# Two-layer hybrid decoder: gating products on another engine, two recurrence heads at priority, weight sums one set at a time

## The chip, the cores and the metric

The kernel runs on one core of a Trainium2 chip. The metric is the time of one execution on the device in microseconds (us). A core has a matrix engine (TensorE, PE), a vector engine (VectorE, DVE), a scalar engine (ScalarE, ACT), a general engine (GpSimd, POOL) and a queue engine that starts transfers (SyncE, SP). Each takes its instructions in the order of the program and waits on semaphores for the others.

## The reference

Two layers on 1024 rows of width 1024. Layer 0 is windowed attention; layer 1 is a gated linear recurrence (HGRN2) with eight heads of 128. The change lies in layer 1:

```python
h = rmsnorm(x, pre_norm_w[layer])
proj = h @ w_in                                   # 1024 x 4096
q, f, i, z = jnp.split(proj, ...)                 # 1024 columns each
q = silu(q)
log_f = logaddexp(log(lb), log1p(-lb) + log_sigmoid(f)); k = -expm1(log_f)
o = chunked_gated_recurrence(q, k, i, log_f)      # per head: state S, 128 x 128
o = o * rsqrt(mean(o * o, -1) + eps) * gnorm_w
o = o * silu(z)                                   # the gate
x = x + rmsnorm(o @ w_out, post_norm_w[layer])
```

## The kernel before

Every fp32 product is three products of split operands (high x high, low x high, high x low), all by `product` (L246). Weights come from DRAM through `fetch` (L162, on SP, four staging tiles `wraw`); `advance` splits each as soon as one of ten slots is free: the high part `whi` on ACT (L203), the low part `wlo` on DVE (L204).

Layer 1 has two parts. `mixer1` projects the values `i` (`i_unit`, halves 0 and 1), and `q` and `f` head by head (`qf_unit`; L946 multiplies `q` by its sigmoid and so empties a PSUM bank), and works the heads off in `rec(h)`: two scans on DVE, scaled copies (L1032, L1035, L1036), scores on PE (`psd`, `pss`, `psq`), transposes that ACT takes from PSUM as `yn` (L1088), products with them (`psk`, L1093), the chain of states `S` on DVE (L1099), the output (`pso`) and its norm.

`final1` computes z and the output projection, each as seven block products (`z1`, `z7`, `z6`, `z4`, `z5`, `z3`, `z2`, and the same for `o`). Four of the seven use sums and differences of weight quarters. These are made in `weight_sums` during `mixer1`, 128 rows at a time: load four quarters `bq`, four operations on DVE, store four results in DRAM (`tz` for z, `td` for the output); there are four sets of each. From there they are fetched like weights. The first z block (`first_part`, into the tiles `p1z`) runs within `mixer1`, ahead of head 7. `gate` multiplies one 128x512 block of the recurrence's output by silu(z): the silu on ACT (L1236), the product on POOL (L1237), 16 times. `turned` transposes the gated blocks on PE (L1208), `split` makes high and low parts for the output projection (ACT L1200, DVE L1201).

The order on each engine is set when the program is built, by a scheduler with a simulated time line, from the order in which `plan` calls the units and from priorities. Instructions of different units are interleaved by it.

Of the kernel before, what the change touches and what calls it, by code (L numbers as in the profile page):

```python
# [12 lines left out]
F32 = mybir.dt.float32  # L13
# [5 lines left out]
ALU = mybir.AluOpType  # L19
# [4 lines left out]
P = 128  # L24
# [66 lines left out]
def emit(tc, I, out):  # L91
    nc = tc.nc
    v = InOrder(tc, nc.vector)
# [7 lines left out]
    with top:  # L101
# [11 lines left out]
        tz, td, sd = [[dp.tile([4 * P, 512], F32, name=f"{n}{i}") for i in range(4)] for n in ("tz", "td", "sd")]  # L113
# [24 lines left out]
        QZ, QO = (100, 108, 104, 112), (120, 128, 116, 124)  # L138
# [15 lines left out]
        W = {"phase": 0, "pos": 0, "bank": 0, "plan": [], "split": 0, "fetch": 0, "left": {}, "place": {}, "dmas": {}, "split_ins": {}, "free": list(zip(whi, wlo))}  # L154
# [767 lines left out]
        def mixer1(fast, vo, rp, p1z):  # L922
            def i_unit(c, t):
                ps = proj_nat(52 if c == 0 else 76, t)
                nc.scalar.activation(vo[c][:, t, :], ps, AF.Copy)
# [8 lines left out]
            def qf_unit(h, isf, half):  # L934
                ps = proj_feat(60 + 4 * h + 2 * isf + 8 * (h // 4), half)
                cs = slice(half * 512, (half + 1) * 512)
                if (h, isf) not in qfk:
                    if isf and fast:
                        qfk[h, 1] = Fs[h % 2]
                    else:  # L940
                        qfk[h, isf] = rp.tile([P, T], F32, tag="qf"[isf], bufs=2 if isf else nb3, name="qf")
                dst = qfk[h, isf][:, cs]
                if not isf:
                    sg = rp.tile([P, 512], F32, tag="sg", bufs=2, name="sg")
                    nc.scalar.activation(sg, ps, AF.Sigmoid)
                    v.tensor_tensor(dst, ps, sg, op=ALU.mult)  # L946
                else:
                    if (h, 2) not in qfk:
                        qfk[h, 2] = rp.tile([P, T], F32, tag="k", bufs=nb3, name="kk")
                    kk = qfk[h, 2][:, cs]  # L950
                    lb, ol = lbt[:, 1, h:h + 1], lbt[:, 0, h:h + 1]
                    nc.scalar.activation(dst, ps, AF.Sigmoid)  # L952
                    nc.scalar.activation(kk, ps, AF.Sigmoid, scale=-1.0)
                    nc.gpsimd.tensor_scalar(dst, dst, ol, lb, op0=ALU.mult, op1=ALU.add)  # L954
                    nc.gpsimd.tensor_scalar(kk, kk, ol, 1.0, op0=ALU.mult, op1=ALU.mult)
# [161 lines left out]
            qf = lambda h: [lambda u=u: qf_unit(h, *u) for u in QF]  # L1117
            iu = lambda c: [lambda t=t: i_unit(c, t) for t in range(8)]

            def weight_sums(k, quarters, dst, neg):  # L1120

                b = [rp.tile([P, 2, 512], F32, tag=t, name="bq") for t in ("yn", "S")]
                b11, b21, b12, b22 = (x[:, i, :] for x in b for i in range(2))
                for q, x in zip(quarters, (b11, b12, b21, b22)):
                    nc.sync.dma_start(x, I["w"][q + k])
                if neg:
                    v.tensor_tensor(b22, b12, b22, op=ALU.subtract)
                else:
                    v.tensor_tensor(b22, b22, b12, op=ALU.subtract)
                v.tensor_tensor(b12, b12, b11, op=ALU.subtract)  # L1130
                v.tensor_tensor(b11, b11, b22, op=ALU.subtract if neg else ALU.add)
                v.tensor_tensor(b21, b21, b11, op=ALU.subtract)
                for d, x in zip(dst, (b22, b11, b21, b12)):
                    nc.sync.dma_start(d[k * P:(k + 1) * P, :], x)

            rc = lambda h: [lambda: rec(h)]

            def with_sums(units, *a):
                ws = [lambda k=k: weight_sums(k, *a) for k in range(4)]
                return units[:1] + ws[:1] + units[1:3] + ws[1:2] + units[3:5] + ws[2:3] + units[5:7] + ws[3:] + units[7:]  # L1140

            def first_parts():
                next_phase()
                for t in range(3):
                    first_part(t, p1z[t])

            plan = iu(0)
            wo = [lambda k=k: weight_sums(k, QO, td, False) for k in range(4)]
            plan = plan[:1] + wo[:1] + plan[1:3] + wo[1:2] + plan[3:5] + wo[2:3] + plan[5:7] + wo[3:] + plan[7:] + qf(0) + ([zeros] if fast else []) + qf(1) + rc(0) + qf(2) + rc(1) + qf(3) + rc(2) + with_sums(iu(1), QZ, tz, True) + rc(3)
            plan += qf(4) + qf(5) + rc(4) + qf(6) + rc(5) + qf(7) + rc(6) + [first_parts] + rc(7)  # L1150
            for u in plan:
                u()
            if fast:
# [23 lines left out]
        def final1(vo, fp, p1z, spare):  # L1177
# [56 lines left out]

            def gate(c, t, z):
                nc.scalar.activation(z, z, AF.Silu)  # L1236
                nc.gpsimd.tensor_tensor(vo[c][:, t, :], vo[c][:, t, :], z, op=ALU.mult)  # L1237

            banks = ["mm", "mm", "s", "s"]

# [13 lines left out]
            for t in range(4):  # L1254
                ps = mm(tag="to"[t % 2])
                part(ps, quad(4, 1), "z4", t, False)

                sg = sgs[t % 2]
                v.tensor_tensor(sg, ps, u3[t], op=ALU.add)
                gate(0, 4 + t, sg)  # L1260
            p53 = []
            for t in range(4):
                p53.append(mm(tag=banks[t]))
                part(p53[t], quad(0, 1), "z5", t, False)

                v.tensor_tensor(u3[t], p53[t], u3[t], op=ALU.add)
                gate(1, 4 + t, u3[t])
                if t > 1:
                    turned(1, (2 * t - 4, 2 * t - 3))
            for t in range(4):  # L1270
                part(p53[t], quad(0, 0), "z3", t, True)

                v.tensor_tensor(p1[t], p53[t], p1[t], op=ALU.add)
                gate(1, t, p1[t])
                if t > 1:
                    turned(1, (2 * t, 2 * t + 1))
# [75 lines left out]
        def network(fast):  # L1352
            keep, oc = layer0()
            with pool("vo", "left") as vp:
                vo = [o0.rearrange("p a (b c) -> p (a b) c", b=2), vp.tile([P, 8, 512], F32, name="vo1")]
                with pool("fin0", "right") as fp:
                    output0(oc, fp, vo[1])
                keep.close()
                with pool("p1z", "right") as zp:
                    p1z = [zp.tile([P, 512], F32, name=f"p1z{t}") for t in range(3)]  # L1360
                    with pool("rec", "left") as rp:
                        final1(vo, rp, p1z, mixer1(fast, vo, rp, p1z))
# [109 lines left out]
```

## Time and profile before

| | us |
|---|---|
| median of three runs | 899.87 (897.39 to 900.57) |
| profiled execution | 900.18 |
| its span (first to last instruction) | 898.4 |
| PE busy | 863.6 (96%) |
| DVE busy | 642.4 (72%) |
| ACT busy | 453.6 (50%) |
| POOL busy | 343.8 (38%) |

Busy times are of the whole span; PE's are pipelined instructions whose ends are modelled. The mean granted clock of PE is 0.986 of full speed. The value projection of layer 1 begins near 400 us, the heads go on to about 755, the z blocks run from about 700 to 800, and the output projection ends the kernel.

### The profile page before, as it was taken

What the parts mean: (1) busy time and instruction counts of PE and PEld (TensorE: products, weight loads), DVE (VectorE), ACT (ScalarE), POOL (GpSimd) and SP (SyncE); (2) the same over time, 40 slices, a digit from 0 to 9 for tenths busy, and PEclk for the clock granted to TensorE, in tenths of its full rate; (3) what the DMA queues carried; (4) which work ended last, traced back from release to release, by engine and by line L of the source; (5) the groups of instructions that cost most, each with busy time, mean ns of one, the idle gap of its engine ahead of it and who ended that gap; (6) DMA issues with size and microseconds to landing.
All of it is one profiled execution on the core that took longest, in us unless ns stands there. A gap on an engine that the chain in (4) does not pass through costs nothing.

```text
span 898.4 us, 14633 instructions
## 1 busy us (share of the span) xinstructions
PE 863.6 (96%) x5166; PEld 716.6 (80%) x5166; DVE 642.4 (72%) x1043; ACT 453.6 (50%) x1143; POOL 343.8 (38%) x491
## 2 busy tenths in 40 slices
PE   6999999999999999999899999999999899996996
PEld 5888888888878788788788888878887688885885
DVE  7998887777898346865488774466767867567885
ACT  5635777767788233843222331343334454574532
POOL 4543545655676203300344422115424421535032
PEclk9999999999999999999999999999999989997999
DMA  9766454322132135447741010670103245312345
GB/s 336 280 197 180 139 167 139 92 80 73 48 98 75 47 95 187 157 163 258 258 147 40 25 49 24 216 253 29 43 25 94 88 149 188 95 59 83 92 124 187
DMA packets 72923, 114.11 MB, mean 127 GB/s; under 512 B 7048, under 2 KB 27144, under 8 KB 72840
## 3 DMA queue, kind: packets, MB, share of 16 engines
q1 hardware_dynamic: 72560, 113.01, 39.2%
q8 instruction: 43, 0.70, 0.3%
q14 instruction: 40, 0.33, 0.1%
q10 hardware_dynamic: 280, 0.07, 0.0%
HBM read 81.76 MB, written 29.46 MB: 124 GB/s over the span
## 4 chain that ended last, share of the span: by engine, by line
PE 74%; DVE 9%; DMA 5%; ACT 4%; POOL 4%; issue 4%; SPq 0%; DVEq 0%; POOLq 0%; ACTq 0%
PE psmm L246 43%; PE psmm L88 17%; PE pss L88 3%; PE pso L88 2%; PE pso L1106 2%; POOL o L1237 2%; DMA bq<-in_w 1%; PE psk L1093 1%; PE pst L88 1%; PE pso L1108 1%; POOL rstd L285 1%; DVE wlo L204 1%; DMA wraw<-tz 1%; ACT whi L203 1%; DMA tz<-bq 1%
## 5 line engine op out<-in xcount | busy, mean ns | idle before, releaser
L246 PE MATMUL psmm<-whi,acth 128*128 128x512 f32 x448 | 177.9, 399 | 1.3 <-DVE y L851 1.3
L246 PE MATMUL psmm<-wlo,acth 128*128 128x512 f32 x448 | 176.1, 393 | 0.0
L246 PE MATMUL psmm<-whi,actl 128*128 128x512 f32 x448 | 174.8, 394 | 0.0
L204 DVE TENSOR_TENSOR wlo<-wraw,whi 128x512 fp32r<-128x512 f32 x144 | 102.2, 724 | 51.8 <-ACT whi L203 46.9
L203 ACT ACTIVATE whi<-wraw 128x512 fp32r<-128x512 f32 x136 | 84.3, 628 | 90.5 <-PE psmm L246 57.9
L88 PE MATMUL psmm<-acth,whi 128*128 128x512 f32 x272 | 110.7, 407 | 1.7 <-ACT whi L88 1.7
L88 PE MATMUL psmm<-acth,wlo 128*128 128x512 f32 x272 | 107.7, 396 | 0.0
L88 PE MATMUL psmm<-actl,whi 128*128 128x512 f32 x272 | 107.3, 395 | 0.2 <-DVE actl L88 0.2
L246 PE MATMUL psmm<-acth,whi 128*128 128x512 f32 x256 | 102.0, 398 | 2.6 <-DVE qf L946 2.6
L246 PE MATMUL psmm<-actl,whi 128*128 128x512 f32 x256 | 101.1, 395 | 0.0
L246 PE MATMUL psmm<-acth,wlo 128*128 128x512 f32 x256 | 100.7, 393 | 0.0
L246 PEld LDWEIGHTS psmm<-whi,acth 128*128 128x128 f32 x448 | 85.0, 190 | 19.4 <-DVE y L851 1.9
L246 PEld LDWEIGHTS psmm<-whi,actl 128*128 128x128 f32 x448 | 84.7, 189 | 17.7
L246 PEld LDWEIGHTS psmm<-wlo,acth 128*128 128x128 f32 x448 | 84.9, 190 | 16.8
L736 ACT ACTIVATE sm<-sm,st 128x129 f32<-128x129 f32 x128 | 49.9, 392 | 26.1 <-DVE st L734 26.0
L88 PEld LDWEIGHTS psmm<-acth,wlo 128*128 128x128 f32 x272 | 51.5, 190 | 11.7 <-DVE wlo L88 0.2
L88 PEld LDWEIGHTS psmm<-acth,whi 128*128 128x128 f32 x272 | 52.0, 191 | 10.3 <-ACT whi L88 2.0
L246 PEld LDWEIGHTS psmm<-acth,whi 128*128 128x128 f32 x256 | 48.4, 189 | 14.1 <-DVE qf L946 4.0
L88 PEld LDWEIGHTS psmm<-actl,whi 128*128 128x128 f32 x272 | 51.9, 191 | 8.7 <-DVE actl L88 0.7
L246 PEld LDWEIGHTS psmm<-acth,wlo 128*128 128x128 f32 x256 | 48.5, 190 | 10.2
L246 PEld LDWEIGHTS psmm<-actl,whi 128*128 128x128 f32 x256 | 48.5, 189 | 9.6
L954 POOL TENSOR_SCALAR gate<-gate,lbt 128x512 f32<-128x512 f32 x16 | 18.5, 1153 | 95.2 <-ACT gate L952 84.6
(334 smaller groups left out, 1773.6 us busy)
## 6 DMA issues: line engine op xcount, KB each, us to landing
wraw<-in_w SPq DMA_DIRECT2D x124, 256.0 KB
QS<-qd SPq DMA_DIRECT2D x16, 512.0 KB
bq<-in_w SPq DMA_DIRECT2D x32, 256.0 KB
xr<-in_x SPq DMA_DIRECT2D x8, 512.0 KB
x1d<-xn SPq DMA_DIRECT2D x8, 512.0 KB
td<-bq SPq DMA_DIRECT2D x16, 256.0 KB
tz<-bq SPq DMA_DIRECT2D x16, 256.0 KB
wraw<-sd SPq DMA_DIRECT2D x16, 256.0 KB
```

Of the source, the lines that this page charges most:

```text
L88: return (lambda *a, **k: self.tc.keep_in_program_order(f(*a, **k))) if self.on else f
L203: nc.scalar.activation(hi, raw, AF.Copy)
L204: W["split_ins"][i] = v.tensor_tensor(lo, raw, hi.bitcast(F32), op=ALU.subtract)
L246: W["mm"] = pe.matmul(ps, a, b, start=(k == first and i == 0), stop=(k == last and i == 2), skip_group_check=first is None)
L285: W["rstd"] = keep(g.tensor_tensor(r, m, nhalf[:, :width], op=ALU.pow))
L736: W["exp"] = nc.scalar.activation(sm[:, h, :], sm[:, h, :], AF.Exp, bias=nm[:, h:h + 1], scale=-1.0, accum_out=dn[:, h:h + 1])
L954: nc.gpsimd.tensor_scalar(dst, dst, ol, lb, op0=ALU.mult, op1=ALU.add)
L1093: nc.tensor.matmul(pk[:, i, :], yn[:, c, :], vt[:, c, hc], start=True, stop=True)
L1106: nc.tensor.matmul(po[:, i, :], sc[:, c, :], vt[:, c, hc], start=True, stop=(c == 0))
L1108: nc.tensor.matmul(po[:, i, :], X[:, c * P:(c + 1) * P], S[:, c, :], start=False, stop=True)
L1237: nc.gpsimd.tensor_tensor(vo[c][:, t, :], vo[c][:, t, :], z, op=ALU.mult)
```

## The change

There are three parts. In `gate` the product goes to DVE. The heads 6 and 7 are built under `tc.high_priority(offset=1200)`, with `first_parts` between them as before. `weight_sums` works on the three tiles `p1z` instead of the tiles of `yn` and `S`, so only three quarters are loaded at first; the fourth goes into the tile of b12 after that has been stored. Each of the eight sets is issued behind the last weight fetch known when it is built (`behind`), and the sets stand elsewhere in the plan: those of z one after each of the projections of heads 1 to 3 and one within the second half of the values, those of the output after that half and after the projections of heads 4 to 6.

```diff
             def weight_sums(k, quarters, dst, neg):
 
-                b = [rp.tile([P, 2, 512], F32, tag=t, name="bq") for t in ("yn", "S")]
-                b11, b21, b12, b22 = (x[:, i, :] for x in b for i in range(2))
-                for q, x in zip(quarters, (b11, b12, b21, b22)):
-                    nc.sync.dma_start(x, I["w"][q + k])
+                b11, b12, b22 = p1z
+                for q, x in zip(quarters, (b11, b12, None, b22)):
+                    if x is not None:
+                        nc.sync.dma_start(x, I["w"][q + k])
...
                 v.tensor_tensor(b12, b12, b11, op=ALU.subtract)
                 v.tensor_tensor(b11, b11, b22, op=ALU.subtract if neg else ALU.add)
+                r = slice(k * P, (k + 1) * P)
+                for d, x in ((3, b12), (0, b22), (1, b11)):
+                    nc.sync.dma_start(dst[d][r], x)
+                b21 = b12
+                nc.sync.dma_start(b21, I["w"][quarters[2] + k])
                 v.tensor_tensor(b21, b21, b11, op=ALU.subtract)
-                for d, x in zip(dst, (b22, b11, b21, b12)):
-                    nc.sync.dma_start(d[k * P:(k + 1) * P, :], x)
+                nc.sync.dma_start(dst[2][r], b21)
...
+            def behind(f, *a):
+
+                with tc.issue_after(W["dmas"][W["fetch"] - 1].ins):
+                    f(*a)
+
+            def ahead(h):
+                with tc.high_priority(offset=1200):
+                    rec(h)
...
+            i1 = iu(1)
+            plan = iu(0) + qf(0) + ([zeros] if fast else []) + qf(1) + wz[:1] + rc(0) + qf(2) + wz[1:2] + rc(1) + qf(3) + wz[2:3]
+            plan += rc(2) + i1[:4] + wz[3:] + i1[4:] + wo[:1] + rc(3) + qf(4) + wo[1:2] + qf(5) + wo[2:3] + rc(4) + qf(6)
+            plan += wo[3:] + rc(5) + qf(7) + [lambda: ahead(6), first_parts, lambda: ahead(7)]
...
             def gate(c, t, z):
                 nc.scalar.activation(z, z, AF.Silu)
-                nc.gpsimd.tensor_tensor(vo[c][:, t, :], vo[c][:, t, :], z, op=ALU.mult)
+                v.tensor_tensor(vo[c][:, t, :], vo[c][:, t, :], z, op=ALU.mult)
```

Below `weight_sums` the lines of the kernel after stand 11 higher.

On ACT, at head 6 of the recurrence, before the change: `yn_6972` is the first eviction of head 6, `whi4` and `whi5` are splits of z weights that come from `tz` (an underscore and a number mark the copy of a tile).

```order
L203 ACTIVATE acth3_0_128<-wraw3_115 128x512
L1175 ACTIVATE pair_7288<-psmm_7301 128x512
L203 ACTIVATE whi4_96<-wraw0_112 128x512
L203 ACTIVATE whi5_97<-wraw1_113 128x512
L1246 ACTIVATE pair_7288<-psmm_7345 128x512
L1088 ACTIVATE yn_6972<-pst_6974 128x512
```

After it the same eviction is `yn_6956`:

```order
L203 ACTIVATE whi8_100<-wraw2_114 128x512
L203 ACTIVATE whi9_101<-wraw3_115 128x512
L952 ACTIVATE gate1_4224<-psmm_6825 128x512
L953 ACTIVATE kk_6792<-psmm_6825 128x512
L1088 ACTIVATE yn_6956<-pst_6958 128x512
L1088 ACTIVATE yn_6956<-pst_6973 128x512
L1111 ACTIVATE jk_6703,oss_6694<-pso_6695 128x128
```

It now stands right behind the projection of head 7 and ahead of `whi4` and `whi5`.

On DVE, at the first set of sums after the change (L1127 to L1137, inside the preparation of head 1):

```order
L1130 TENSOR_TENSOR p1z1_4210<-p1z1_4210,p1z0_4209 128x512
L1062 TENSOR_TENSOR qf_4482<-qf_4482,tt_4740 128x8x64
L1036 TENSOR_TENSOR qf_4617<-qf_4617,tt_5056 128x32x16
L1032 TENSOR_TENSOR U_5050<-qf_4617,tt_5056 128x32x16
L1035 TENSOR_TENSOR V_5051<-kk_4646,tt_5056 128x32x16
L1030 TENSOR_TENSOR tt_5056<-tt_5056 128x16
L1131 TENSOR_TENSOR p1z0_4209<-p1z0_4209,p1z2_4211 128x512
L1030 TENSOR_TENSOR tt_5056<-tt_5056 128x8
L1137 TENSOR_TENSOR p1z1_4210<-p1z1_4210,p1z0_4209 128x512
```

Between L1130, whose result is stored, and L1137, which needs the tile loaded anew, stand seven other instructions. Before the change the four operations of a set stood nearly or quite together.

On DVE, at the last gated block after the change: the train of splits and sums, which began 18 instructions ahead of the first row here with the split `actl4_1`, and in it the last gate (L1248).

```order
L204 TENSOR_TENSOR wlo8_110<-wraw0_112,whi8_100 128x512
L1212 TENSOR_TENSOR actl1_1_123<-vo1_3486,acth1_1_122 128x512
L1299 TENSOR_TENSOR vo1_3486<-vo1_3486,pair_7284 128x512
L1212 TENSOR_TENSOR actl7_0_145<-pair_7282,acth7_0_144 128x512
L1319 TENSOR_TENSOR pair_7284<-pair_7284,pair_7282 128x512
L204 TENSOR_TENSOR wlo9_111<-wraw1_113,whi9_101 128x512
L1248 TENSOR_TENSOR o0_148<-o0_148,pair_7272 128x512
L1212 TENSOR_TENSOR actl3_1_131<-vo1_3486,acth3_1_130 128x512
```

The gate starts as the 24th instruction behind that split; before the change it was on POOL (L1237), beside this train.

## Rows read from the trace of the kernel before

**Rows 1.** Page, part 1: busy time, share of the span, instructions, by engine.

```profile
PE 863.6 (96%) x5166; PEld 716.6 (80%) x5166; DVE 642.4 (72%) x1043; ACT 453.6 (50%) x1143; POOL 343.8 (38%) x491
```

**Rows 2.** Waits of PE, 390 to 900: us in total, times, longest.

```profile
PE pst L1208 <- POOL o L1237: 7.7, 1, 7.7
PE psk L1093 <- ACT yn L1088: 5.4, 2, 4.8
PE psmm L246 <- DVE qf L946: 2.6, 2, 2.4
PE pso L1106 <- DVE S L1099: 1.4, 2, 1.0
```

**Rows 3.** Windows of PE: us, busy (x), granted clock, DMA share, GB/s.

```profile
446.00:452.00 6.00, 6.00 (x21) 0.72 0.87 261
700.00:705.00 5.00, 5.00 (x24) 1.00 0.28 88
718.00:724.00 6.00, 4.81 (x29) 0.53 0.66 217
821.20:826.00 4.80, 4.74 (x13) 0.50 0.16 52
```

**Rows 4.** Time line of PE: start, us, instruction, idle before.

```profile
812.99 0.39 PE L246 MATMUL psmm<-wlo,acth 128*128 128x512 f32 x1
813.22 0.39 PE L246 MATMUL psmm<-whi,actl 128*128 128x512 f32 x1
821.26 1.11 PE L1208 MATMUL pst<-cst,o 128*128 128x128 f32 x4 [7.65 <-POOL o L1237]
```

**Rows 5.** Chain that ended last, 806 to 826: start, us, what.

```profile
807.50 13.71 POOL o L1237
```

**Rows 6.** Groups of POOL by shape, 750 to 825: busy, mean ns, idle before.

```profile
L1237 POOL TENSOR_TENSOR vo<-vo,pair 128x512 f32<-128x512 f32 x7 | 9.5, 1369 | 6.0 <-ACT pair L1236 5.8 <-PE psmm L246 0.2
```

**Rows 7.** Time line of DVE, 796 to 826.

```profile
818.80 0.68 DVE L1201 TENSOR_TENSOR actl<-vo,acth 128x512 fp32r<-128x512 f32 x1
819.40 0.68 DVE L204 TENSOR_TENSOR wlo<-wraw,whi 128x512 fp32r<-128x512 f32 x1
824.74 0.69 DVE L1201 TENSOR_TENSOR actl<-pair,acth 128x512 fp32r<-128x512 f32 x1 [4.66 <-ACT acth L1200]
```

**Rows 8.** Windows of DVE, columns as in rows 3.

```profile
455.00:560.00 105.00, 79.04 (x118) 1.00 0.14 45
603.00:690.00 87.00, 63.89 (x96) 1.00 0.13 40
757.00:797.80 40.80, 20.90 (x30) 1.00 0.35 112
797.80:820.10 22.30, 22.26 (x35) 0.90 0.25 71
```

**Rows 9.** Time line of ACT, 708 to 726.

```profile
716.90 1.27 ACT L203 ACTIVATE whi<-wraw 128x512 fp32r<-128x512 f32 x2 [6.31 <-DMA wraw<-tz]
...
718.55 0.59 ACT L1088 ACTIVATE yn<-pst 128x512 f32<-128x512 f32 x1
```

**Rows 10.** Time line of DVE, 440 to 447.

```profile
441.13 0.69 DVE L1129 TENSOR_TENSOR bq<-bq 128x512 f32<-128x512 f32 x1 [4.26 <-DMA bq<-in_w]
```

**Rows 11.** Chain that ended last, 660 to 692.

```profile
677.38 4.18 PE psmm L246 x17
```

**Rows 12.** Time line of DVE, 658 to 682.

```profile
680.70 0.68 DVE L1035 TENSOR_TENSOR V<-kk,tt 128x512 f32<-128x512 f32 x1
```

**Rows 13.** Chain that ended last, 564 to 606.

```profile
568.99 2.02 DMA tz<-bq
571.08 4.39 DMA bq<-in_w
```

**Rows 14.** Groups of DVE by shape, 395 to 700.

```profile
L1032 DVE TENSOR_TENSOR U<-qf,tt 128x512 f32<-128x512 f32 x7 | 8.2, 1168 | 0.0
```

**Rows 15.** Waits of SP, 380 to 700: us in total, times, longest.

```profile
SPq L162 <- DVE wlo L204: 123.9, 30, 21.2
```

More of the change, by code (lines that the diff above doesn't have):

```diff
@@ L1131, in weight_sums @@
                 v.tensor_tensor(b11, b11, b22, op=ALU.subtract if neg else ALU.add)
+                r = slice(k * P, (k + 1) * P)
[3 more added lines that the diff above has]
+                nc.sync.dma_start(b21, I["w"][quarters[2] + k])
                 v.tensor_tensor(b21, b21, b11, op=ALU.subtract)
-                for d, x in zip(dst, (b22, b11, b21, b12)):
-                    nc.sync.dma_start(d[k * P:(k + 1) * P, :], x)
+                nc.sync.dma_start(dst[2][r], b21)
             rc = lambda h: [lambda: rec(h)]
-            def with_sums(units, *a):
-                ws = [lambda k=k: weight_sums(k, *a) for k in range(4)]
-                return units[:1] + ws[:1] + units[1:3] + ws[1:2] + units[3:5] + ws[2:3] + units[5:7] + ws[3:] + units[7:]
+            wz, wo = ([lambda k=k, q=q, d=d, n=n: behind(weight_sums, k, q, d, n) for k in range(4)] for q, d, n in ((QZ, tz, True), (QO, td, False)))
+            def behind(f, *a):
[4 more added lines that the diff above has]
+                    rec(h)
             def first_parts():
@@ L1145, in first_parts @@
                     first_part(t, p1z[t])
[L1147 to L1150, printed above, removed]
+            i1 = iu(1)
+            plan = iu(0) + qf(0) + ([zeros] if fast else []) + qf(1) + wz[:1] + rc(0) + qf(2) + wz[1:2] + rc(1) + qf(3) + wz[2:3]
+            plan += rc(2) + i1[:4] + wz[3:] + i1[4:] + wo[:1] + rc(3) + qf(4) + wo[1:2] + qf(5) + wo[2:3] + rc(4) + qf(6)
+            plan += wo[3:] + rc(5) + qf(7) + [lambda: ahead(6), first_parts, lambda: ahead(7)]
             for u in plan:
```

## The prediction

> **What bounds the kernel now.** I began with the page. TensorE (PE) is busy 863.6 of the 898.4 us [rows 1], so the change can pay only where PE stands still, or runs at a lower clock, and only in the stretch that it touches, from about 390 us on. I therefore asked next what PE waits for from 390 to 900. The list is short [rows 2]: one wait of 7.7 us on the gate on GpSimd (POOL), two on the eviction `yn` (4.8 and 0.6), two on `qf` (2.4 and 0.2), two on `S` (1.0 and 0.4). The 0.6 and the 0.2 lie at 601 to 623, behind the second group of sums. The third view is PE's windows around the three long waits [rows 3]. After each the granted clock falls to 0.50 of full speed, the 1.2 GHz level, for some microseconds: on average 0.50 from 821.2 to 826, 0.53 from 718 to 724, 0.72 from 446 to 452. After the 1.0 us on `S`, which ended at 695, it is not: 1.00 from 700 to 705. So a long wait costs itself and then some.
>
> What stands behind each wait:
>
> The 7.7 us. PE has done the products ahead of the last four transposes by 813.6 and starts these at 821.26 [rows 4]; they need the last gated block. The chain gives 13.71 us to that one gate on POOL, begun at 807.50 [rows 5], where seven others of the same shape take 1369 ns [rows 6]. VectorE (DVE) runs back to back from 797.8 to 820.1 (22.26 of 22.30 us busy) and then rests 4.66 us [rows 7, 8]. The gate ends at 821.2, 1.1 us after that rest began: it got through only when DVE went idle.
>
> The Trainium skill, "SBUF — State Buffer", "Who interferes with whom", says that a VectorE instruction with two SBUF inputs and a GpSimd one that reads SBUF contend for one shared pair, which whoever issued first keeps for the whole instruction. The trace agrees that the two interfere (13702 against 1369 ns), but not that one DVE instruction is the unit of the wait.
>
> The 4.8 us. ScalarE (ACT) issues in order. Two splits `whi` stand idle 6.31 us until 716.90 for weights from `tz`, and behind them stands the eviction `yn` of head 6, at 718.55 [rows 9], for which PE waits.
>
> The 2.4 us. DVE's sums of the output weights wait for loads (4.26 us idle ahead of the one at 441.13 [rows 10]), and `qf` (L946), which empties a PSUM bank, runs behind them.
>
> **The change part by part.**
>
> *Gates.* Sixteen products leave POOL for DVE. DVE does 128x512 with two SBUF inputs in 0.68 us, one every 0.60 back to back [rows 7], so 16 x 0.68 = 11 us of DVE. From 757 to 797.8, where most of the gates fall, DVE has 40.8 - 20.9 = 19.9 us to spare [rows 8]; so these are covered. In the train after 797.8 nothing is to spare, but there the place in the order counts: the last gate stands 24 instructions behind the split that starts the train (the order's last block), so it starts at 797.8 + 24 x 0.60 = 812.2 and ends at 812.9. PE comes to its four transposes at 813.6 plus three products now put ahead of them (one every 0.23 us [rows 4]), 814.3. The 7.7 us go, and with them the slow products: 4.8 us at 0.50, 2.4 us. Two gates now lie in the train, 1.2 us. What PE needs next from it is `actl2_1`, 31 instructions behind its start: 797.8 + 18.6 + 0.7 = 817.1. PE wants it 28 products after the four transposes (about 0.9 us): 814.3 + 0.9 + 28 x 0.23 = 821.6. I book 0.5 us of new loss for this stage, between 0 and the whole 7.7.
>
> *Priority of heads 6 and 7.* `yn` of head 6 now stands ahead of the splits that wait for `tz` (ACT's rows). The 4.8 us go. So does the slow clock: 0.47 of 4.8 us busy, 2.2 us [rows 3]. Price: the first scores of head 6 (`psd`) stand fifteen products into a projection that begins at 677.38, so PE is there at 677.4 + 15 x 0.227 = 680.8, while DVE's L1035, which they need, ends at 680.70 + 0.68 = 681.4 [rows 11, 12]. That is 0.6 us; 1.1 if PE comes earlier by the two short waits ahead. I take 1.1. The state chain `S` of head 6 is woven into splits that wait for `tz`, as before the 1.0 us at 694: 0 to 1.5, I take 0.7.
>
> *Sums.* Same number of loads, operations and stores (32 of each, operations of 0.69 us [rows 10]), spread over 460 to 680 instead of two bunches. The output group leaves the window at 440: its 2.4 us go, and the slow clock with them, 0.28 of 6.0, 1.7 us [rows 3]. The second group leaves the path to the wait at 601, where the chain goes from a store of 2.02 us to a load of 4.39 us [rows 13]: 0.8 us. New is a step inside each set: the third operation's tile is stored, loaded again, and only then is the fourth operation possible. Store and load one after the other are at most 2.02 + 4.39 = 6.4 us, and 4.0 if the load of the same size is as quick as the store. On DVE four to six instructions of a head's preparation (such as L1032, 1.17 us [rows 14]) mostly stand between; what is left waits with DVE in order, and behind it stand splits, `qf` and `S`. DVE has 26 us free of 105 from 455 to 560, and 23 of 87 from 603 to 690 [rows 8]. The worst place is the fourth set of the gate weights, directly behind the third on the same tiles: both loads lie open, some 5 + 3 us of DVE, with PE in the value projection, whose bank evictions are ACT's. I book 0.7 us, between 0 and 4. The weights fetched behind a set on SP wait for its stores and its reload. I cost that at nothing: SP already stands 123.9 us of the 320 from 380 to 700 waiting for splits before it may fetch [rows 15], and the DMA engines are used 13 to 14% in the quiet stretches [rows 8]; without this cover it is the first rival below.
>
> *Sum.* Gone: waits 7.7 + 4.8 + 2.4 + 0.8 + 1.0 (the wait at 694, replaced by the 0.7 below) = 16.7; slow clock 2.4 + 2.2 + 1.7 = 6.3; together 23.0. New: 0.5 + 1.1 + 0.7 + 0.7 = 3.0. The profiled execution took 900.18 us (span 898.4), 0.3 above the median of the three runs, 899.87; I work from it: 900.2 - 23.0 + 3.0 = 880.2. I say **880 us**. The likeliest case runs from 876 (new losses at their lower ends, and a little off the short waits) to 885 (4 us of new waits that also cost clock).
>
> **The rivals.**
>
> *The sums take the time back in part.* The reload stalls PE at some of the eight sets. For it: DVE issues in order, and at 443 such a wait did reach PE. Against it: in most sets the preparation of a head stands between store and fourth operation. Two or three sets at 2.4 us, plus 1.7 us of clock each, as at 443, make 8 to 12 us: 888 to 892; four would make 896.
>
> *The sums make it slower.* The same at every set: 8 x (2.4 + 1.7) = 33 us, up to 8 x (4.4 + 2) = 51 if PE sits out the whole load. Less the 23: 910 to 928. It decides from 23/8 = 2.9 us per set on. Against it: PE waited 2.4 us in all four sets of the output group together, although all of those had their loads open on DVE [rows 2, 10].
>
> *The gate comes late on DVE as well.* If the train starts late or is fuller, by 8 us (the 16 gates' 9.6 us not covered at all), the gate ends at 822 and the 10.1 us stay: 890.
>
> *The gate is not what the contention cost.* By a rule that a transfer through the shared pair waits for one DVE instruction only, the gate on POOL would have ended at 807.5 + 0.7 + 1.4 = 809.6, before PE's 813.6, and the 13.7 us would have another cause which the move leaves in place: 880 + 10.1, 890. The row speaks against it: POOL ends 1.1 us after DVE's first rest, nearly the length of an undisturbed gate.
>
> That is the Trainium skill's rule on that page ("Issue order, not op shape, decides who blocks") taken to the letter.
>
> *The new order does not do what it says.* If head 6 is not ahead in time, because `psd` is late by more than the booked 1.1 us, 7 us stay: 887.
>
> **How the numbers follow.** Chances: the forecast 0.66; partly taken back by the sums 0.13; gate late 0.07; gate not the cause 0.03; order not effective 0.05; slower 0.04; no net change from several of these 0.02. The predicted time is the likeliest case's, 880. The range goes from 873 (876 less 3 us of short waits that vanish too) to 892, which takes in the partial rivals; outside lie the slower case and the ends of the others, some 0.12. Within 0.5% (4.5 us, about what a measurement of this kernel can tell from no change: three runs spread over 3.2) lie the last case and the upper end of the partial ones, 0.06; slower 0.04; the rest, 0.90, is faster.
>
> **What would show it.** In the profile after: no wait of PE on L1248 (the gate) over 1 us, and DVE's last gate ending near 813 less the 10 us gained before it, about 803; PE's clock 1.00 in those slices; `yn` of head 6 not behind a wait of ACT; no wait on L946 near 440. The sum is wrong if PE's list of waits shows L946 or `S` behind L1137 at several sets, or a new wait on L1212 in the last 90 us; right if total waits from 390 on come to 3 to 5 us.

## The result and the profile after

The changed kernel takes 891.14 us (median of five runs, 890.59 to 893.01) against 899.87; the ratio is 0.9914, 95% interval 0.9893 to 0.9934. It is faster, by 8.7 us and not by 20. The profiled execution has a span of 889.0 us:

The page's first part, busy time by engine:

```profile
span 889.0 us, 14613 instructions
PE 861.7 (97%) x5166; PEld 715.4 (80%) x5166; DVE 645.7 (73%) x1059; ACT 453.9 (51%) x1143; POOL 313.5 (35%) x475
```

What PE waits for from 390 to 900 (us in total, times, longest):

```profile
PE psq L1070 <- DVE qf L1062: 3.1, 1, 3.1
PE psmm L246 <- DVE qf L946: 2.8, 4, 1.5
PE psmm L246 <- ACT o L1221: 1.3, 1, 1.3
PE pso L1106 <- DVE S L1099: 1.0, 1, 1.0
PE psd L1044 <- DVE tt L1030: 0.2, 1, 0.2
```

The three long waits of [rows 2] are gone, all three. Waits of 8.4 us stand in the list now, where 17.1 stood; the forecast had booked 3.0 us of new losses. The longest is new. PE's windows (columns as in rows 3) at the places of the old long waits and at the new one:

```profile
440.00:452.00 12.00, 12.00 (x54) 1.00 0.19 64
677.00:680.00 3.00, 3.00 (x38) 0.54 0.00 0
700.00:735.00 35.00, 35.00 (x297) 1.00 0.44 133
805.00:830.00 25.00, 23.72 (x110) 1.00 0.39 118
```

The clock is 1.00 where it was 0.50 to 0.72 in [rows 3]. Between 390 and PE's last products it is low in this execution only behind the new wait: 0.46 of 3 us, 1.4 us of slow products.

That new wait begins on DVE. Its time line from 659 to 677 (start, us, instruction, and in brackets the idle time before it):

```profile
660.34 0.69 DVE L1129 TENSOR_TENSOR p1z<-p1z,p1z 128x512 f32<-128x512 f32 x1 [3.21 <-DMA p1z<-in_w]
661.06 1.15 DVE L1130 TENSOR_TENSOR p1z<-p1z,p1z 128x512 f32<-128x512 f32 x1
662.24 1.06 DVE L1131 TENSOR_TENSOR p1z<-p1z,p1z 128x512 f32<-128x512 f32 x1
663.23 0.21 DVE L1009 COPY F<-gate 128x64 f32<-128x64 f32 x1
668.51 0.69 DVE L1137 TENSOR_TENSOR p1z<-p1z,p1z 128x512 f32<-128x512 f32 x1 [5.07 <-DMA p1z<-in_w]
669.12 0.68 DVE L1114 TENSOR_TENSOR vo<-pso,rstd 128x512 f32<-128x512 f32 x1
669.72 2.28 DVE L1013 TENSOR_TENSOR_SCAN U<-gate,F 128x1024 f32<-128x1024 f32 x1
671.91 2.27 DVE L1014 TENSOR_TENSOR_SCAN V<-gate,E 128x1024 f32<-128x1024 f32 x1
674.10 1.80 DVE L1048 COPY_PREDICATED sc<-msk,psd 32x256 f32<-32x256 uint8 x4
675.93 0.69 DVE L1062 TENSOR_TENSOR qf<-qf,tt 128x512 f32<-128x512 f32 x1
```

This is the last of the eight sets. Its fourth operation (L1137) waits 5.07 us for the quarter that is loaded anew, and the chain gives the reason as one store and one load in a row:

```profile
662.24 2.01 DMA td<-p1z
...
664.30 4.11 DMA p1z<-in_w
```

Behind L1137 stand the scans of head 6 (L1013, L1014) and L1062 of head 5, which PE's `psq` needs. So DVE's wait for a transfer arrives at PE as 3.1 us. It is not the only set that waits. Of DVE's waits from 455 to 690, L1137 has (us in total, times, longest):

```profile
DVE p1z L1137 <- DMA p1z<-in_w: 14.4, 4, 5.1
```

Four of the eight sets stand idle before their fourth operation, and the last one longest.

### The profile page after: what moved, and what is told of

The parts are those of the page before. It is cut to its first block, busy times and chain, and to the rows that moved or that the text cites. A ratio compares the mean times of both kernels' runs of the same rounds, so it can differ in the third digit from the quotient of the medians.

```text
span 889.0 us, 14613 instructions
## 1 busy us (share of the span) xinstructions
PE 861.7 (97%) x5166; PEld 715.4 (80%) x5166; DVE 645.7 (73%) x1059; ACT 453.9 (51%) x1143; POOL 313.5 (35%) x475
## 4 chain that ended last, share of the span: by engine, by line
PE 69%; DVE 16%; DMA 4%; issue 4%; ACT 3%; POOL 2%; SPq 0%; DVEq 0%; POOLq 0%; ACTq 0%
PE psmm L246 39%; PE psmm L88 17%; PE pss L88 3%; PE pso L88 2%; DMA p1z<-in_w 2%; PE pso L1106 2%; PE pst L88 1%; PE pso L1108 1%; DVE U L1013 1%; PE psk L1093 1%; POOL rstd L285 1%; DVE sc L1048 1%; DVE V L1014 1%; DVE kk L1016 1%; DVE qf L1015 1%
## 5 line engine op out<-in xcount | busy, mean ns | idle before, releaser
L204 DVE TENSOR_TENSOR wlo<-wraw,whi 128x512 fp32r<-128x512 f32 x144 | 99.0, 700 | 64.4 <-ACT whi L203 63.7
L246 PEld LDWEIGHTS psmm<-acth,whi 128*128 128x128 f32 x256 | 48.3, 189 | 14.4 <-DVE qf L946 4.4
L246 PEld LDWEIGHTS psmm<-acth,wlo 128*128 128x128 f32 x256 | 48.3, 189 | 10.1
```

Source lines behind the costliest of these rows:

```text
L204: W["split_ins"][i] = v.tensor_tensor(lo, raw, hi.bitcast(F32), op=ALU.subtract)
L246: W["mm"] = pe.matmul(ps, a, b, start=(k == first and i == 0), stop=(k == last and i == 2), skip_group_check=first is None)
```

## The experiments

### Each part alone

The gate alone:

```diff
-                nc.gpsimd.tensor_tensor(vo[c][:, t, :], vo[c][:, t, :], z, op=ALU.mult)
+                v.tensor_tensor(vo[c][:, t, :], vo[c][:, t, :], z, op=ALU.mult)
```

> The kernel before with one edit: the 16 gating products on VectorE. Theory A (read from the trace after): the 7.7 us wait and the 2.4 us of slow products go, and about 1.4 us of waiting for the last transposed block comes in their place, so 8.7 us less: about 891.3. Rival (the last gate's 13.7 us had another cause, which stays): no change, 898 to 901. The record's own step said 10.1 - 0.5 = 9.6 us, about 890.5.

Measured: 891.63 us, ratio 0.9919 (0.9900 to 0.9939), against 899.43 for the kernel before on the same chip: 7.8 us less. PE's waits from 700 to 890, where the gate's 7.7 us stood:

```profile
PE psk L1093 <- ACT yn L1088: 4.7, 1, 4.7
PE psmm L246 <- ACT o L1210: 1.3, 1, 1.3
```

The gate was the cause of its wait. 1.3 us for the eviction of the last transposed block came in its place. The wait on `qf` near 443 has changed as well, though nothing there was edited: in this run's list from 390 on, L946 has 1.9 us and its longest is 1.6, not 2.4. That is no effect of the gate: the kernel before shows as little in other executions (see the part on why the prediction was wrong).

The priority alone:

```diff
-... + rc(5) + qf(7) + rc(6) + [first_parts] + rc(7)
+... + rc(5) + qf(7) + [lambda: ahead(6), first_parts, lambda: ahead(7)]
```

> The kernel before with one edit: heads 6 and 7 at priority. Theory A: the 4.8 us wait on yn and 2.2 us of slow clock go, but on PE the short products of head 7 (pss, psq) now alternate with psk and pso of head 6, nine times instead of twice, at about 0.35 us for each there and back: some 3 us come in, net 4 us less, about 896, with no wait in PE's list for the 3 us. Rival (the record's steps): 7.0 gone, 1.1 + 0.7 new, 5.2 us less: about 895, no loss outside the list of waits. The time hardly tells them apart; the gaps between PE's products at the two places do.

Measured: 893.39 us, 0.9941 (0.9919 to 0.9964): 6.0 us less, more than either theory had. The 4.8 us on `yn` are gone (0.2 remain).

The sums alone (the changed kernel with the gate on POOL and `rc(6)`, `rc(7)` as before):

> The kernel before with one edit: the weight sums on the tiles p1z, one set at a time, with the fourth quarter loaded anew. Theory A: the waits at 443 and 601 go (some 5 us with the clock), but the sets' instructions and reloads in order on DVE bring in about 10 us between 440 and 690, nearly half of it where the last set waits 5 us for its fourth quarter ahead of head 6's scan and PE waits 3.1 us for psq: net 4 to 5 us more, 904 to 905. Rival (the record's steps): 5 us gone, 0.7 new: 895 to 896.

Measured: 905.07 us, 1.0077 (1.0050 to 1.0104): 5.6 us *more*. PE's waits of this kernel from 390 on:

```profile
PE pst L1219 <- POOL o L1248: 7.7, 1, 7.7
PE psk L1093 <- ACT yn L1088: 4.6, 1, 4.6
PE psmm L246 <- DVE qf L946: 4.4, 5, 1.5
PE psq L1070 <- DVE qf L1062: 3.1, 1, 3.1
PE pso L1106 <- DVE S L1099: 2.5, 2, 1.6
```

Against [rows 2]: L946 has 1.8 us more, `S` 1.1 more, and the 3.1 us on `psq` are new. Theory A's time is met, and this is where the missing gain is. The three parts add up: -7.8 - 6.0 + 5.6 = -8.2, and together they gave -8.7.

### Two of the three

Gate and priority, with the sums as before:

> The kernel before with two of the three edits: gating products on VectorE, heads 6 and 7 at priority; the weight sums as before. Theory A (the three edits add up, and the sums' edit is a loss): 7.8 + 6.0 us off the kernel before, about 885.6, some 5 us below the changed kernel. Rival (the sums' edit costs only where it stands alone, with the gate on GpSimd and head 6 late; in company it is level): 890 to 892, like the changed kernel.

Measured: 885.09 us (884.42 to 886.28), 0.9843 (0.9825 to 0.9861). The parts add, the rival falls, and this kernel is better than both. With the old sums, in the order that the other two edits lead to, PE waits 1.5 us for L946 in four pieces (the first two lines of its list):

```profile
PE psmm L246 <- DVE qf L946: 1.5, 4, 0.7
PE psmm L246 <- ACT o L1214: 1.3, 1, 1.3
```

### Inside the sums

The last set's fourth operation behind the preparation of head 6 (`fourth` holds that operation and its store, `prep` is L1035 of the head built last):

```diff
+            def last_fourth():
+                with tc.issue_after(W["prep"].ins):
+                    fourth(slice(3 * P, 4 * P), p1z[1], p1z[0], td[2])
...
+[lambda: ahead(6), last_fourth, first_parts, lambda: ahead(7)]
```

> The changed kernel with one instruction elsewhere: the last set's fourth operation (and its store) is issued behind the preparation of head 6 and not ahead of its scans. Theory A (the reload in front of head 6's scans costs PE 3.1 us of wait and 1.2 us of slow clock, about 4.7 in all): 886 to 887. Rival (VectorE is so full there that the work is late anyway): 890 to 891.

Measured: 887.68 us, 0.9870 (0.9850 to 0.9890), 3.5 us below the changed kernel, most of the 4.7 that theory A named. The wait on `psq` is 0.2 us in place of 3.1. Head 6's first scan starts at 666.61, and what DVE waits for there is now the norm of head 4's output:

```profile
666.00 0.69 DVE L1114 TENSOR_TENSOR vo<-pso,rstd 128x512 f32<-128x512 f32 x1 [1.69 <-POOL rstd L285]
666.61 2.28 DVE L1013 TENSOR_TENSOR_SCAN U<-gate,F 128x1024 f32<-128x1024 f32 x1
```

All four operations of all eight sets left out, loads and stores kept:

> The changed kernel with the four operations of each of the eight sets left out; the loads, reloads and stores stay, so the products use unsummed weights. Theory A (all that the sums' edit costs comes through VectorE's queue: the wait for reloads and 32 operations among the heads' preparation): PE's waits on psq, on qf and on S between 470 and 690 go but for about 1 us, 8 us less: about 883. Rival (a good part comes through SP and the DMA queues, weights fetched late): 887 to 890, with waits of PE on splits that wait for fetches.

Measured: 879.85 us, 0.9791 (0.9769 to 0.9813), 11.3 us below the changed kernel. PE's list from 390 on is short:

```profile
PE psmm L246 <- ACT o L1214: 1.3, 1, 1.3
PE psd L1044 <- DVE tt L1030: 0.7, 1, 0.7
PE psk L1093 <- DVE vo L1114: 0.4, 1, 0.4
PE psmm L246 <- DVE qf L946: 0.2, 1, 0.2
```

There is no wait for a split that waits for a fetch, although SP carries the same transfers in the same sets. So what the sums cost goes through DVE's queue, as theory A had it. Waiting and arithmetic were taken out together here, so their shares are not shown; and since the kernel before does the same 32 operations, the 11.3 us are more than the edit alone costs (6.0 us, the changed kernel against gate and priority). The time came out 3 us better than theory A said: of the 11.3 us, 7.1 are waits in the changed kernel's list (3.1, 2.8, 1.0 and 0.2) and 1.4 the slow products, less 1.3 us of waits that this kernel still has beside the eviction of the last block. Of the other 4 us the two traces place most: 0.6 lie ahead of 390 and 1.1 behind PE's last product, where the two kernels are alike, and about 1 between the first scores and the last outputs of heads 6 and 7, where PE goes back and forth less often between short and long products (ten short groups of `pss` and `psq` in place of 14; the next section has the price).

### Head 7 at ordinary priority, and what an alternation costs

With both heads at priority, PE does the short products of head 7 between those of head 6. Its time line in the changed kernel:

```profile
712.76 0.22 PE L1054 MATMUL pss<-qf,kk 128*32 128x32 f32 x2
712.91 0.49 PE L1093 MATMUL psk<-vo,yn 128*128 128x128 f32 x2
713.33 0.25 PE L1054 MATMUL pss<-qf,kk 128*32 128x32 f32 x2
713.50 0.49 PE L1093 MATMUL psk<-vo,yn 128*128 128x128 f32 x2
```

One there and back, of one product each, takes 0.59 us (712.91 to 713.50), without any wait in PE's list. The edit:

```diff
-[lambda: ahead(6), first_parts, lambda: ahead(7)]
+[lambda: ahead(6), first_parts] + rc(7)
```

> The changed kernel with head 7 at ordinary priority; head 6 stays ahead. On PE pss and psq of head 7 then no longer alternate with psk and pso of head 6. Theory A (each there and back costs PE about 0.35 us, 13 of them): 4 us less than the changed kernel, about 887. Rival (the alternation costs nothing of its own, PE does the same products): the same, 891, or more because head 7 comes later.

Measured: 892.52 us, 0.9935 (0.9912 to 0.9957). The gain did not come; the rival is right about the time. The alternation is gone from the order, but between two products of head 6's output PE now waits for `S`:

```profile
721.48 0.63 PE L1070 MATMUL psq<-qf,kk 128*32 128x64 f32 x26
724.58 0.49 PE L1106 MATMUL pso<-vo,sc 128*128 128x128 f32 x2 [2.47 <-DVE S L1099]
```

This trace is of the fastest of the four executions (889.43 us, mean granted clock 0.998); the other three took 892.1 to 893.85 us at 0.994, so they had slow products besides.

To see the price by itself, products on constants were added behind the end of the kernel before (`bigs` of 128x128, `smalls` with 32 columns on either side):

```diff
+            bigs(32)
+            smalls(32)
+            for i in range(16):
+                bigs(2)
+                smalls(2)
```

> The kernel before with products added behind its last ones, on constants and read by nobody: 32 of 128x128 in a row, 32 of 32x32 in a row, then 16 times two and two. Theory A (changing between the two shapes costs PE time): the rows give about 3.5 and 0.4 us for the two runs, and 16 x 0.6 = 9.5 us for the same work alternated, 0.35 us for each there and back. Rival (PE does them at the same pace): about 4 us.

PE's time line; each product counts as two instructions:

```profile
889.93 7.31 PE L1358 MATMUL big<-cst 128*128 128x128 f32 x64
897.17 0.76 PE L1362 MATMUL small<-cst 128*32 128x32 f32 x64
897.86 0.71 PE L1358 MATMUL big<-cst 128*128 128x128 f32 x4
898.50 0.26 PE L1362 MATMUL small<-cst 128*32 128x32 f32 x4
898.69 0.71 PE L1358 MATMUL big<-cst 128*128 128x128 f32 x4
```

In a row, two of the one and two of the other take 4 x 0.113 + 4 x 0.011 = 0.50 us (7.24 and 0.69 us for 64 instructions each). Alternated they take 0.83 (897.86 to 898.69): 0.33 us more for each there and back. The run of 32 took 7.2 us and not the 3.5 that I had put down, because I had taken instructions for products; the price of the change is as expected. So the alternation costs, an estimated 4 us for 13 of them at 0.33, and what it buys in the changed kernel is that PE's wait for `S` is filled. The same edit on the kernel with gate and priority:

> Like the kernel with gate and priority, but head 7 at ordinary priority. Theory A (the alternation on PE costs some 3.6 us, but without it PE waits for the states S of head 6 instead, as in the run with the changed kernel): 884 to 887, the same as with both heads at priority. Rival (the alternation is pure loss): 881 to 882.

Measured: 884.98 us, 0.9833 (0.9800 to 0.9866): the same as with both heads at priority, as theory A had it. Its reason holds only in part: in this trace PE waits 1.2 us for the norm `vo` (L1114) and 0.5 for `S` near 710, not 2.5 for `S`.

### Why the gate took 13.7 us on GpSimd

Products of VectorE behind the end of the kernel before, and one on GpSimd released by a copy on VectorE (`two` has both inputs in SBUF, `one` has one in PSUM):

```diff
+            def phase(*train):
+                keep(v.tensor_copy(wraw[2], side))
+                keep(nc.gpsimd.tensor_tensor(sgs[1], wraw[2], wraw[3], op=ALU.mult))
+                for f, n in train:
+                    f(n)
+            phase((two, 24))
+            phase((one, 24))
+            phase((two, 8), (one, 1), (two, 16))
+            phase((two, 8), (one, 4), (two, 16))
+            phase()
+            phase()
```

> The kernel before with work added behind its last instructions, read by nobody: a 128x512 product on GpSimd, released by a copy on VectorE, beside trains of VectorE products of the same shape: (1) 24 with both inputs in SBUF, (2) 24 with one input in PSUM, (3) 8 and 16 with two SBUF inputs around a single one with a PSUM input, (4) the same around four such, (5) alone, twice. Theory A (the product on GpSimd gets through only when VectorE has no instruction with two SBUF inputs, so the 13.7 us are the train's): 16 us in (1), 1.3 to 1.4 us in (2) and (5), about 6 to 7 us in (4), and in (3) 6 to 17 us. Rival (it waits for one VectorE instruction only): about 2 us in all of them.

The rival was right here. The product took 1.67 us in case (1), 1.30 in (2), 1.64 in (3), 1.65 in (4) and 1.26 alone. But these trains were not like the one in the kernel: all products wrote the same tile, and one came every 0.72 us, behind the end of the last. So I ran it with four result tiles in turn:

> As in the run on the ports, but VectorE's products go round among four result tiles, so that one may begin before the last has ended (one every 0.60 us, as in the train before the last gate), and each product on GpSimd is released from within a train: (1) ahead of 24 with four tiles, (2) ahead of 24 into one and the same tile (one every 0.72 us in the earlier run), (3) ahead of 24 with a PSUM input, (4) ahead of 8, then 4 with a PSUM input, then 16, (5) alone. Theory A (VectorE's instructions hold the way to SBUF as long as each begins before the last ends): about 15 us in (1), 1.3 to 1.7 in (2), 1.3 in (3) and (5), 6 to 8 in (4). Rival (GpSimd gets through behind one VectorE instruction in any train, and the 13.7 us of the gate had a cause of their own): 1.3 to 2 us in all five.

The five products on GpSimd:

```profile
899.00 15.49 POOL L1369 TENSOR_TENSOR sg<-wraw,wraw 128x512 f32<-128x512 f32 x1 [9.95 <-DVE wraw L1368]
915.29 1.67 POOL L1369 TENSOR_TENSOR sg<-wraw,wraw 128x512 f32<-128x512 f32 x1 [0.81 <-DVE wraw L1368]
939.06 1.29 POOL L1369 TENSOR_TENSOR sg<-wraw,wraw 128x512 f32<-128x512 f32 x1 [22.11 <-DVE wraw L1368]
954.01 1.64 POOL L1369 TENSOR_TENSOR sg<-wraw,wraw 128x512 f32<-128x512 f32 x1 [13.65 <-DVE wraw L1368]
972.51 1.26 POOL L1369 TENSOR_TENSOR sg<-wraw,wraw 128x512 f32<-128x512 f32 x1 [16.86 <-DVE wraw L1368]
```

In case (1), beside a train with one instruction every 0.60 us, the product waits the train out: 15.49 us, as the last gate did. Beside instructions that begin only when the last has ended it takes 1.67 us, and beside products with one SBUF input 1.29, about as alone. Case (4) went against theory A: 1.64 us, though its first eight also came every 0.60 us; VectorE gave way once, and its three instructions there took 2.95 us in place of 1.88. Cases (1) and (4) also differ in what VectorE did just ahead of the release (in (1) products with two SBUF inputs, in (4) products with one in PSUM) and in the length of the train, and each was measured once. So overlap is not shown to be the whole condition, and what decides who gives way stays open. That the gate's place on GpSimd was the cause of PE's 7.7 us does not hang on it: the run with the gate alone shows that.

The Trainium skill, "SBUF — State Buffer", "Who interferes with whom", gives the shared pair to whoever issued first for the whole of that instruction; read to the letter, the other then waits for one. Cases (2) and (4) agree with it (1.67 and 1.64 us); case (1) does not (15.49 us), and the measurement decides.

## Why the prediction was wrong

What the three parts were to bring, by the terms of the sum, beside what each brought alone:

| part | forecast | alone |
|---|---|---|
| gate: -10.1 + 0.5 | -9.6 | -7.8 |
| priority: -7.0 + 1.1, and 0.7 for 1.0 | -6.2 | -6.0 |
| sums: -2.4 - 1.7 - 0.8 + 0.7 | -4.2 | +5.6 |

**The gate** was right in mechanism and nearly in size. The last gate starts on DVE 14.4 us behind the split that opens the train, which is 24 x 0.60, and PE does not wait for it (it is at 810.31 and not at the 803 that the prediction named as a sign, because only 2 us of the 10 had been gained by then):

```profile
795.87 0.69 DVE L1212 TENSOR_TENSOR actl<-vo,acth 128x512 fp32r<-128x512 f32 x1 [0.98 <-ACT acth L1211]
...
810.31 0.69 DVE L1248 TENSOR_TENSOR o<-o,pair 128x512 f32<-128x512 f32 x1
```

PE's four transposes start at 812.19 without a wait. Too small was the 0.5 us for the rest of the stage: the eviction of the transposed block, which PE waits for, cost 1.3.

**The priority** came out as booked, in part by luck: two things that I had not seen cancel. PE's short products alternate, and without that PE waits in the same place (2.5 us for `S` in the changed kernel, 1.2 for `vo` and 0.5 for `S` with gate and priority), so the alternation cost nothing net. The wait on `psd`, booked at 1.1 us, is 0.2 in the changed kernel and 0.5 to 0.7 in the other runs with head 6 at priority.

**The sums** are the step that failed: 9.8 of the 11.3 us by which the sum was off. "I book 0.7 us, between 0 and 4" was wrong in place and in size. The fourth operation waited for its reload in four of the eight sets, 14.4 us on DVE. I took the fourth set of the gate weights for the worst place. DVE stood idle there about as the prediction said (4.7 and 3.4 us, up to 558.28), and it cost PE the 1.0 us on `S`, which DVE works on from 558.89. The worst was the fourth set of the output weights, where DVE waited 5.07 us and between the third operation and the fourth there stands not a head's preparation but one short copy (L1009), with the scans of head 6 behind; the order showed it, and I had read one set for all. (The tile that is stored and loaded anew is that of the second operation, L1130, and not of the third, as the prediction has it.)

Against gate and priority the edit of the sums costs 6.0 us; putting that one operation later gave 3.5 of them back. The remaining 2.6 go with L946 and `S`: PE waits 4.1 and 0.8 us for them with that operation late, 1.5 and none with gate and priority, 0.2 and none without the arithmetic. Not all of it is reloads: the longest wait on L946 (1.5 us) ends at 510, where on DVE two operations of a set (L1127 and L1130, without a wait) stand ahead of L946. DVE's free time, 26 us of 105 and 23 of 87 [rows 8], was no cover: DVE still had 23.2 us free of the 105 from 455 to 560 in the changed kernel, while PE waited for it.

What was to go was booked too high as well. The 4.1 us at 443 (2.4 of wait, 1.7 of slow clock) were those of one execution. Three of the runs above are the kernel before with work added only behind its end; in them PE's wait on L946 at that place is (products, then the two runs on GpSimd):

```profile
444.65 0.50 PE L246 MATMUL psmm<-acth,whi 128*128 128x512 f32 x1 [1.23 <-DVE qf L946]
445.40 0.50 PE L246 MATMUL psmm<-acth,whi 128*128 128x512 f32 x1 [1.69 <-DVE qf L946]
443.90 0.50 PE L246 MATMUL psmm<-acth,whi 128*128 128x512 f32 x1 [1.20 <-DVE qf L946]
```

From 446 to 452 the clock is 1.00 in all three, where [rows 3] has 0.72. So three of four traces of the unchanged kernel lose 1.2 to 1.7 us there and not 4.1. The runs with the gate alone (1.6) and the priority alone (1.0) lie as low, at a clock of 1.00. A second trace of the same kernel would have shown it.

The rival "the sums take the time back in part" named the mechanism, in-order DVE, and gave it 0.13 and 888 to 892. The time came out at the upper end of that rival, and not near the forecast's own 876 to 885.

## What to carry to other kernels

An operation that waits for a transfer on an in-order engine costs by what stands behind it there. Read the order at every instance of a repeated step, the last above all; the engine's mean idle time says nothing about it. A load into a tile that must first be stored puts two transfers in a row (2.0 + 4.1 us here), so put other work of that engine between by hand where the scheduler's order does not. Read a short wait in more than one execution before you book it as a gain. And measure the parts of a composite change one by one: here two of three gave 14.4 us and the third took 6 back.

## What was not expected of the hardware

A change between products of 128x128 and of 32 columns costs PE 0.33 us there and back, with no wait in the trace. A GpSimd product of two SBUF inputs may wait 15.49 us beside VectorE instructions that overlap (one every 0.60 us at 0.68 us each); it took 1.67 beside the same instructions when each begins only behind the end of the last, and 1.64 in one train that did overlap. And a wait of a given length does not settle PE's clock: behind 2.4 us in the kernel before [rows 2, 3] it fell to 0.50 for some microseconds, behind 2.8 and 2.5 us in the profiled run with head 7 at ordinary priority it stayed at 1.00.
